# Tiles at other addresses in a decoder trunk: stationary operands at the high end of the large buffers, starts at multiples of 128 bytes

## The chip, the cores and the metric

The kernel runs on one core of a Trainium2 chip. A core has a matrix engine (TensorE, PE in the rows), a vector engine (VectorE, DVE), an activation engine (ScalarE, ACT), GpSimd (POOL) and a queue engine (SyncE, SP) that issues the transfers. They share an on-chip memory of 128 partitions. A tile occupies the same byte range in each partition; its address below is its first byte in the partition. Matmuls write into a second memory, PSUM. The metric is the device time of one execution in microseconds, lower is better.

## The reference

Two layers over 256 tokens of width 1024. Each layer has a feed-forward half, a token mixer and a second feed-forward half, each behind a norm that is shifted, scaled and gated by a vector c:

```python
for l in range(DEPTH):
    mod = (c_act @ w_ada[l] + b_ada[l]).reshape(B, 3, 3, D_MODEL)
    h = ada_norm(x, norm_g[l, 0], mod[:, 0, 0], mod[:, 0, 1])
    x = x + 0.5 * mod[:, 0, 2][:, None, :] * swiglu(h, ffn_w13[l, 0], ffn_w2[l, 0])
    h = ada_norm(x, norm_g[l, 1], mod[:, 1, 0], mod[:, 1, 1])
    x = x + mod[:, 1, 2][:, None, :] * token_mixer(h, w_in[l], ..., w_out[l], cos, sin)
    h = ada_norm(x, norm_g[l, 2], mod[:, 2, 0], mod[:, 2, 1])
    x = x + 0.5 * mod[:, 2, 2][:, None, :] * swiglu(h, ffn_w13[l, 1], ffn_w2[l, 1])
return rms_norm(x, final_g)
```

swiglu is (silu(h @ a) * (h @ b)) @ w2 with an inner width of 2816. token_mixer projects h once, runs three kinds of attention over 16 heads and projects the result back to 1024. All of it is in float32.

## The kernel before

**Products in three parts.** A float32 product is computed from operands that are each split into a high and a low part in the format float32r: hi*hi + hi*lo + lo*hi, three matmuls into the same PSUM bank (`mm3`). Of the activations the split, transposed tiles are the stationary operand: `hThi0`, `hTlo0` for the first 128 tokens (t = 0), `hThi1`, `hTlo1` for the second (t = 1), 8 chunks of 128 columns each, and `gThi`, `gTlo` (three buffers of each, 2 chunks of 128) for the gated inner values. Weights are the moving operand: a chunk of 128 x 1024 is loaded into `raw` (7 buffers), ScalarE copies it to `whi` and VectorE subtracts to `wlo` (8 buffers of each).

**Feed-forward.** The inner width is cut into 11 groups j. `G1(j, t, ks)` multiplies h by a group's two halves, 512 columns, over 8 chunks k; `act` applies silu and the gate; `TR` transposes the result into gThi/gTlo; `G2` multiplies by w2 into y. In the steady loop the tokens alternate inside k:

```python
def steady(j):
    for k in K8:
        for t in range(NT):
            G1(j, t, [k])
    ...
    for f in range(2):
        for t in range(NT):
            G2(j - 1, t, (f,))
    for t in range(NT):
        TR(j, t)
```

So 48 matmuls of G1 take t = 0 and t = 1 in threes by turns, 24 of G2 follow, then four transposes. The last group (`end`) has `G1(j, 1, K8[2:])`, 18 matmuls at t = 1 alone.

**Mixer.** `proj(name, t, K8)` multiplies h by six groups of columns, five of 512 and one (`nv`) of 284, 24 matmuls for each t, and `oproj` projects back (six of its eight chunks from the hT tiles, two from gT tiles). The first projection of the mixer is `proj("ka", 0, K8)`, at t = 0 alone.

**Other names.** `onesr` is a stationary tile of ones that spreads a gate row over the partitions (`mod_part`); `ident` is the moving operand of transposes; `crow` is a row of c by which `raw` is multiplied and summed in `columns`.

**Order.** The code is recorded once, a scheduler fixes each engine's order and every buffer from its own costs and a table of offsets, and the code is run a second time to issue it. Every recorded instruction therefore has one line, that of the issuing loop.

**Place.** `Program.tile` makes a tile at its first use, and the pool lays tiles one behind the other in the order in which they are made. So the order of first use in the code sets the addresses. A tile's size is a multiple of 32 bytes, and small tiles between the large ones move all that follow off the multiples of 128. The built programs place (first byte in the partition; in brackets what is left over from a multiple of 128):

```
                   before                  after
onesr              26688 (64)              25728 (0)
crow               41216 (0)               40192 (0)
hThi0, hTlo0       62112, 66208 (32)       202240, 206336 (0)
raw, 7 buffers     70304 to 98976 (32)     60928 to 89600 (0)
whi, 8 buffers     101216 to 133984 (96)   91648 to 124416 (0)
wlo, 8 buffers     133984 to 166752 (96)   124416 to 157184 (0)
hThi1, hTlo1       174944, 179040 (96)     210432, 214528 (0)
gThi, 3 buffers    187232 to 190304 (96)   218624 to 221696 (0)
gTlo, 3 buffers    190304 to 193376 (96)   221696 to 224768 (0)
nq0, nq1           193376, 197472 (96)     169472, 173568 (0)
ms, 4 buffers      214560 to 220704 (32)   189952 to 196096 (0)
pt, 4 buffers      222208 to 228352 (0)    196096 to 202240 (0)
```

Of the kernel before, what the change touches and what calls it, by code (L numbers as in the profile page):

```python
# [7 lines left out]
F32 = mybir.dt.float32  # L8
F32R = mybir.dt.float32r
# [277 lines left out]
class Program:  # L287
# [9 lines left out]
            k.made = []  # L297

    def tile(self, pool, shape, dt, name, bufs=1, loose=False, psum=False):
        if name not in self.kinds:  # L300
            self.kinds[name] = Kind([pool.tile(shape, dt, name=f"{name}_{i}" if bufs > 1 else name)
                                     for i in range(bufs)], loose)
        kind = self.kinds[name]
        b = Buf(len(self.bufs), kind, psum)
        self.bufs.append(b)
        return View(b, kind.tiles[self.plan[1][b.i] if self.plan else 0])
# [298 lines left out]
GROUPS1 = [2, 2, 2, 1, 1]  # L605
NRAW, NHL, NMS, NPT = 7, 8, 4, 4
S0, S1 = 21, 33


@with_exitstack  # L610
# [1186 lines left out]
```

## Time and profile before

| | |
|---|---|
| median of 3 runs | 1066.04 us (1064.94 to 1066.87) |
| profiled execution, its time | 1065.23 us |
| its span, first to last instruction | 1063.5 us |
| TensorE busy | 1041.4 us |
| VectorE busy | 830.9 us |
| ScalarE busy | 603.3 us |
| bytes moved | 257.97 MB |

The span is what the rows below cover; the time of the same execution is 1.7 us longer, and the median of the runs another 0.8 us. A matmul's row gives its start and a modelled end, and matmuls overlap: the distance between two starts is what a matmul takes from the engine, not the duration in its row.

### The profile page before, as it was taken

To read this page: it belongs to the slowest core of one execution; us is meant where nothing else is said; L and a number is where in the kernel's file an instruction comes from. 1 tells how busy PE (TensorE), PEld (TensorE's weight loads), DVE (VectorE), ACT (ScalarE), POOL (GpSimd) and SP (SyncE) were. 2 spreads that over 40 slices of the span, in tenths; PEclk is the share of its full clock that TensorE was granted. 3 is DMA by queue.
4 is the path that set the end of the run, shared out by engine and by line. 5 is a ranking of instruction groups with operands and counts; after the bars stand their busy time and mean duration, and the time that the engine had idled before them with its cause. 6 is when DMAs were issued, how large, how long until landed. Compare 5 with 4: busy or idle time off the path is not lost.

```text
span 1063.5 us, 14643 instructions
## 1 busy us (share of the span) xinstructions
PE 1041.4 (98%) x5060; PEld 838.7 (79%) x5060; DVE 830.9 (78%) x1561; ACT 603.3 (57%) x1094; POOL 27.7 (3%) x63
## 2 busy tenths in 40 slices
PE   5999999999999999999999999999999999999997
PEld 3888888888777788788888888887877788888885
DVE  6999988779998887788587667758999778556554
ACT  5564354567887644535485444447677766444442
POOL 3000000000000100000000000000000010000000
PEclk9999999999999999999999999999999999999999
DMA  9999999567663698899548777854758247666611
GB/s 341 371 324 367 377 337 327 191 206 243 204 227 123 223 339 318 291 339 336 198 168 283 256 268 257 284 210 154 236 180 264 93 149 277 210 206 210 209 65 39
DMA packets 71468, 257.97 MB, mean 243 GB/s; under 512 B 8193, under 2 KB 8193, under 8 KB 71394
## 3 DMA queue, kind: packets, MB, share of 16 engines
q1 hardware_dynamic: 70850, 256.12, 68.8%
q0 software_dynamic: 544, 0.93, 0.4%
q8 instruction: 39, 0.64, 0.2%
q14 instruction: 35, 0.29, 0.1%
HBM read 255.96 MB, written 1.05 MB: 242 GB/s over the span
## 4 chain that ended last, share of the span: by engine, by line
PE 87%; DVE 7%; DMA 2%; ACT 2%; issue 1%; POOL 1%; SPq 0%; POOLq 0%; DVEq 0%; ACTq 0%
PE ps_pc L561 51%; PE ps_pa L561 15%; PE ps_pb L561 14%; PE ps_tr L561 7%; DVE wlo L561 3%; DMA raw<-in_w_dram 2%; DMA x<-in_x_dram 1%; ACT whi L561 1%; DVE raw L561 1%; DVE nf L561 0%; POOL ss L561 0%; DVE u L561 0%; ACT xn L561 0%; DVE hTlo L561 0%; SPq L561 0%
## 5 line engine op out<-in xcount | busy, mean ns | idle before, releaser
L561 DVE TENSOR_TENSOR wlo<-raw,whi 128x1024 fp32r<-128x1024 f32 (+1 forms) x342 | 410.8, 1216 | 129.0 <-ACT whi L561 127.4
L561 ACT ACTIVATE whi<-raw 128x1024 fp32r<-128x1024 f32 (+1 forms) x342 | 356.7, 1053 | 200.1 <-PE ps_pc L561 107.6
L561 PE MATMUL ps_pc<-whi,hThi 128*128 128x512 f32 (+1 forms) x872 | 347.6, 399 | 0.4 <-ACT gates L561 0.3
L561 PE MATMUL ps_pc<-whi,hTlo 128*128 128x512 f32 (+1 forms) x872 | 340.7, 391 | 0.0
L561 PE MATMUL ps_pc<-wlo,hThi 128*128 128x512 f32 (+1 forms) x872 | 340.5, 390 | 0.0
L561 PEld LDWEIGHTS ps_pc<-whi,hThi 128*128 128x128 f32 x872 | 163.9, 188 | 37.2 <-issue 1.8
L561 PEld LDWEIGHTS ps_pc<-whi,hTlo 128*128 128x128 f32 x872 | 163.7, 188 | 36.7 <-DVE hTlo L561 0.2
L561 PEld LDWEIGHTS ps_pc<-wlo,hThi 128*128 128x128 f32 x872 | 164.0, 188 | 33.3
L561 DVE CUSTOM_DVE_ANT_0 raw<-raw,crow 128x1024 f32<-128x1024 f32 x96 | 115.6, 1221 | 7.2 <-DMA raw<-in_wada_dram 7.2
L561 ACT ACTIVATE gThi<-ps_tr 128x256 fp32r<-128x256 f32 x88 | 32.7, 383 | 74.4 <-PE ps_tr L561 74.2
L561 ACT ACTIVATE sg<-ps_pc 128x256 f32<-128x256 f32 x82 | 31.5, 384 | 75.8 <-PE ps_pc L561 75.5
L561 PE MATMUL ps_pa<-whi,gThi 128*128 128x512 f32 x184 | 73.5, 399 | 0.0
L561 PE MATMUL ps_pb<-whi,gThi 128*128 128x512 f32 x176 | 72.4, 411 | 0.0
L561 PE MATMUL ps_pa<-whi,gTlo 128*128 128x512 f32 x184 | 72.0, 391 | 0.0
L561 PE MATMUL ps_pa<-wlo,gThi 128*128 128x512 f32 x184 | 71.8, 390 | 0.0
L561 PE MATMUL ps_pb<-whi,gTlo 128*128 128x512 f32 x176 | 69.1, 393 | 0.0
L561 PE MATMUL ps_pb<-wlo,gThi 128*128 128x512 f32 x176 | 68.7, 390 | 0.0
L561 DVE SCALAR_TENSOR_TENSOR gate<-raw,cact,gate 128x1024 f32<-128x1024 f32 x48 | 61.4, 1279 | 6.6 <-DMA raw<-in_wada_dram 6.6
L561 ACT ACTIVATE ms<-ms,nm 128x128 f32<-128x128 f32 (+1 forms) x96 | 42.6, 446 | 16.5 <-DVE nm L561 16.5
L561 DVE TENSOR_TENSOR gg<-ps_pc,sg 128x256 f32<-128x256 f32 x82 | 33.5, 420 | 20.8 <-ACT sg L561 19.6
L561 DVE TENSOR_TENSOR gTlo<-ps_tr,gThi 128x256 fp32r<-128x256 f32 x88 | 36.0, 420 | 16.9 <-ACT gThi L561 16.9
L561 PEld LDWEIGHTS ps_pa<-whi,gTlo 128*128 128x128 f32 x184 | 34.5, 188 | 7.5
(257 smaller groups left out, 1085.8 us busy)
## 6 DMA issues: line engine op xcount, KB each, us to landing
raw<-in_w_dram SPq DMA_DIRECT2D x264, 512.0 KB, 4.9
raw<-in_wada_dram SPq DMA_DIRECT2D x144, 512.0 KB, 4.8
raw<-in_win_dram SPq DMA_DIRECT2D x40, 512.0 KB, 4.3
raw<-in_wc_dram SPq DMA_DIRECT2D x16, 512.0 KB, 3.5
raw<-in_wout_dram SPq DMA_DIRECT2D x16, 512.0 KB, 5.1
raw<-in_win_dram SPq DMA_DIRECT2D x4, 426.0 KB, 3.1
x<-in_x_dram SPq DMA_DIRECT2D x2, 512.0 KB, 6.6
out_dram<-xn SPq DMA_DIRECT2D x4, 256.0 KB, 2.1
```

Of the source, the lines that this page charges most:

```text
L561: return getattr(self.eng, op)(*[plain(a) for a in args], **{k: plain(v) for k, v in kw.items()})
```

## The change

All large tiles are made at once, at the first use of any of them, in the order of a list `HOMES`; small tiles follow when they are first used. Since every size in the list is a multiple of 128 bytes, or stands where the next still starts on one, each of the listed tiles starts at a multiple of 128. The transposed inputs (hThi0, hTlo0, hThi1, hTlo1) and the gated tiles (gThi, gTlo) are last in the list, so they lie above all the others. The instructions of each engine, their order and the buffer numbers that they use are the same in both programs.

```diff
     def tile(self, pool, shape, dt, name, bufs=1, loose=False, psum=False):
+        if name not in self.kinds and name in HOMES:
+
+            for n, (s, d, b) in HOMES.items():
+                self.kinds[n] = Kind([pool.tile(s, d, name=f"{n}_{i}" if b > 1 else n) for i in range(b)], False)
         if name not in self.kinds:
...
+HOMES = {
+    "x0": ([128, 1024], F32, 1), "x1": ([128, 1024], F32, 1), "ones": ([128, 128], F32, 1),
...
+    "raw": ([128, 1024], F32, 7), "nf": ([128, 256], F32, 2), "whi": ([128, 1024], F32R, 8),
+    "wlo": ([128, 1024], F32R, 8), "tk": ([128, 4, 512], F32, 1), "sg": ([128, 256], F32, 2),
...
+    "rb": ([128, 8, 16], F32, 1), "ms": ([128, 384], F32, 4), "pt": ([128, 384], F32, 4),
+    "hThi0": ([128, 8, 128], F32R, 1), "hTlo0": ([128, 8, 128], F32R, 1), "hThi1": ([128, 8, 128], F32R, 1),
+    "hTlo1": ([128, 8, 128], F32R, 1), "gThi": ([128, 2, 128], F32R, 3), "gTlo": ([128, 2, 128], F32R, 3),
+}
```

## Rows read from the trace of the kernel before

**Rows 1.** The page's first part: span and busy time of each engine.

```profile
span 1063.5 us, 14643 instructions
...
PE 1041.4 (98%) x5060; PEld 838.7 (79%) x5060; DVE 830.9 (78%) x1561; ACT 603.3 (57%) x1094; POOL 27.7 (3%) x63
```

**Rows 2.** The page's fourth part: the chain that ended last, by engine.

```profile
PE 87%; DVE 7%; DMA 2%; ACT 2%; issue 1%; POOL 1%; SPq 0%; POOLq 0%; DVEq 0%; ACTq 0%
```

**Rows 3.** Chain from 610 to 725 us: start us, us, engine and output, matmuls merged.

```profile
619.88 11.15 PE ps_pc L561 x48
631.03 1.37 PE ps_pa L561 x6
...
633.76 1.36 PE ps_pa L561 x6
...
636.49 0.44 PE ps_tr L561 x4
636.93 11.15 PE ps_pc L561 x48
```

**Rows 4.** The chain from 190 to 235 us, the same columns.

```profile
191.81 1.39 PE ps_pa L561 x6
...
193.42 1.38 PE ps_pc L561 x6
194.80 4.08 PE ps_pa L561 x18
198.88 4.08 PE ps_pc L561 x18
...
216.59 5.60 PE ps_pc L561 x24
```

**Rows 5.** The chain from 1030 us to the end.

```profile
1046.14 4.08 PE ps_pc L561 x18
```

**Rows 6.** TensorE's timeline near 209 us: start us, duration, instruction, merged count.

```profile
209.40 1.09 PE L561 MATMUL ps_tr<-nq,onesr 128*128 128x512 f32 x4
210.33 0.40 PE L561 MATMUL ps_pc<-whi,hThi 128*128 128x512 f32 x1
```

**Rows 7.** Groups of one tile (hThi, then gThi): count, duration min/median/max ns.

```profile
L561 PE MATMUL ps_pc<-whi,hThi x872: 288/393/578, 27.5 to 1049.4; 128*128 128x512 f32 x168, 128*128 128x284 f32 x7
...
L561 PE MATMUL ps_pa<-whi,hThi x40: 389/389/628, 17.8 to 865.4; 128*128 128x512 f32 x40
...
L561 PE MATMUL ps_tr<-whi,hThi x16: 389/394/775, 17.2 to 59.0; 128*128 128x512 f32 x16
...
L561 PE MATMUL ps_pb<-whi,hThi x16: 389/393/482, 22.0 to 62.5; 128*128 128x512 f32 x16
...
L561 PE MATMUL ps_pa<-whi,gThi x184: 389/389/481, 64.0 to 1045.3; 128*128 128x512 f32 x184
...
L561 PE MATMUL ps_pb<-whi,gThi x176: 389/389/481, 66.9 to 1055.1; 128*128 128x512 f32 x176
...
L561 PE MATMUL ps_pc<-whi,gThi x8: 393/474/587, 323.4 to 849.4; 128*128 128x512 f32 x8
```

**Rows 8.** Stretches: length, busy us of each engine (count), clock, DMA share, GB/s.

```profile
20.00:205.00 185.00, 185.00 (x828) 149.69 (x827) 168.55 (x273) 90.37 (x131) 0.55 (x1) 1.00 0.93 342
205.00:350.00 145.00, 143.54 (x854) 115.21 (x853) 131.56 (x369) 112.63 (x272) 4.87 (x6) 1.00 0.59 195
...
535.00:725.00 190.00, 190.00 (x857) 154.97 (x856) 134.05 (x181) 98.31 (x145) 2.10 (x4) 1.00 0.72 244
725.00:860.00 135.00, 133.57 (x807) 105.55 (x806) 117.51 (x353) 101.66 (x250) 3.08 (x4) 1.00 0.53 174
```

**Rows 9.** Groups that write or read raw: count, duration min/median/max ns, forms.

```profile
L561 ACT ACTIVATE whi<-raw x342: 681/1060/1097, 15.1 to 1032.6; 128x1024 fp32r<-128x1024 f32 x169, 128x852 fp32r<-128x852 f32 x2
L561 DVE TENSOR_TENSOR wlo<-raw,whi x342: 731/1221/1228, 16.6 to 1033.6; 128x1024 fp32r<-128x1024 f32 x168, 128x852 fp32r<-128x852 f32 x2, 128x568 fp32r<-128x568 f32 x1
...
L561 DVE CUSTOM_DVE_ANT_0 raw<-raw,crow x96: 1174/1219/1445, 8.9 to 810.8; 128x1024 f32<-128x1024 f32 x96
```

More of the change, by code (lines that the diff above doesn't have):

```diff
@@ L607 @@
 S0, S1 = 21, 33
+HOMES = {
+    "x0": ([128, 1024], F32, 1), "x1": ([128, 1024], F32, 1), "ones": ([128, 128], F32, 1),
+    "ident": ([128, 128], F32, 1), "onesr": ([128, 128], F32R, 1), "mask": ([128, 384], F32, 1),
+    "lower": ([128, 128], F32, 1), "cmask": ([128, 2, 16], F32, 1), "vals": ([128, 2, 12, 64], F32, 1),
+    "fqk": ([128, 2, 8, 66], F32, 1), "kcT": ([128, 2, 16], F32, 1), "kcs": ([128, 2, 2, 16], F32R, 1),
+    "hexp": ([128, 2, 4, 2, 16], F32, 1), "crow": ([128, 1024], F32, 1), "gate": ([128, 1024], F32, 2),
+    "cs": ([128, 2, 2, 16], F32, 1), "xn": ([128, 1024], F32, 1), "zbmo": ([128, 4, 256], F32, 1),
+    "raw": ([128, 1024], F32, 7), "nf": ([128, 256], F32, 2), "whi": ([128, 1024], F32R, 8),
+    "wlo": ([128, 1024], F32R, 8), "tk": ([128, 4, 512], F32, 1), "sg": ([128, 256], F32, 2),
+    "gg": ([128, 256], F32, 2), "nq0": ([128, 4, 256], F32R, 1), "nq1": ([128, 4, 256], F32R, 1),
+    "u": ([128, 512], F32, 2), "nk0": ([128, 2, 256], F32R, 1), "nk1": ([128, 2, 256], F32R, 1),
+    "vbd": ([128, 8, 64], F32, 1), "wc2": ([128, 256], F32, 1), "ra": ([128, 8, 16], F32, 1),
+    "rb": ([128, 8, 16], F32, 1), "ms": ([128, 384], F32, 4), "pt": ([128, 384], F32, 4),
+    "hThi0": ([128, 8, 128], F32R, 1), "hTlo0": ([128, 8, 128], F32R, 1), "hThi1": ([128, 8, 128], F32R, 1),
+    "hTlo1": ([128, 8, 128], F32R, 1), "gThi": ([128, 2, 128], F32R, 3), "gTlo": ([128, 2, 128], F32R, 3),
+}
 @with_exitstack
```

## The prediction

> **What bounds the kernel now.** I read the busy shares first: TensorE is busy for 1041.4 of 1063.5 us, VectorE for 830.9 and ScalarE for 603.3 [rows 1]. A busy TensorE may still have gaps that its modelled ends hide, so I went on to the chain of work that ended last. It runs through TensorE for 87% of the span [rows 2]. So the time is made of the distances from one matmul to the next, and the question is what sets such a distance. No row has it directly, but the chain merges matmuls that follow each other without a wait into one piece with a count. The length of a piece divided by its count is the mean distance.
>
> The steady loop of the feed-forward blocks shows two levels side by side. The 48 matmuls of G1 take 11.15 us, 232.3 ns each. The matmuls of G2 that follow, six to a piece, take 1.36 or 1.37 us, 227 to 228 ns each [rows 3]. Both kinds have the same shape: 128 rows of weights, 512 moving columns, the same moving tiles whi and wlo. At the full clock, 2.4 GHz, 512 columns would alone be 213 ns. The clock was granted fully in every stage listed [rows 8].
>
> What differs is the stationary operand. G1 uses hThi0/hTlo0 and hThi1/hTlo1 by turns (t alternates inside k), G2 uses gThi/gTlo. Where the program uses one of them alone, the levels come apart. The 24 matmuls of the mixer's first projection at t = 0 take 5.60 us, **233.3 ns** each. The 18 at t = 1 in the end of the first feed-forward block (G1(j, 1, K8[2:])) take 4.08 us, **226.7 ns** each. The 18 of G2 just before them also take 4.08 us, 226.7 ns [rows 4]. The end of the last block shows the same 4.08 us for 18 at t = 1, 850 us later [rows 5]. Code, shape and moving tiles are the same for t = 0 and t = 1; the data and the place of the stationary tiles are not. By the placement table hThi0 and hTlo0 lie at 62,112 to 70,304 bytes of a partition, hThi1 and hTlo1 at 174,944 to 183,136, and gThi and gTlo at 187,232 to 193,376. A third low tile agrees: onesr, at 26,688, is the stationary operand of four matmuls that take 0.93 us from the first start to the next instruction's start, 232.5 ns each [rows 6]. Two other pieces show that the fast level is not reached at once. The first six matmuls of G2 after a t = 0 stretch take 1.39 us (231.7 each), the first six at t = 1 behind transposes 1.38 us (230 each) [rows 4].
>
> **The change, part by part.** No instruction is added, taken away or moved; every tile gets another address. I cost this by kind of tile.
>
> *Stationary tiles.* All twelve go to 202,240 to 224,768 bytes, above the tiles that are fast now. Counts: matmuls with whi and hThi are 872 + 40 + 16 + 16 = 944 [rows 7], and each comes with one of wlo and hThi and one of whi and hTlo, 2832 in all. Of these 96 have 284 columns (eight chunks, two t, two layers, three each), which leaves 2736 of 512 columns, 1368 for each t. With gThi there are 184 + 176 + 8 = 368 [rows 7], so 1104. In the program's own order 676 of the t = 0 matmuls have no t = 1 matmul among the three wide matmuls before them, 692 have one; 802 of the t = 1 matmuls have a t = 0 one there, 566 have none. The 676 run at 233.3 ns, the 692 + 802 at the mixed 232.3 ns. If all of them settle at the 226.7 ns that the high tiles show, the change gives 676 x 6.6 ns = 4.5 us and 1494 x 5.6 ns = 8.4 us, **12.8 us** together. The 566 and the 1104 are there already: nothing.
>
> *Settling.* After transposes or other small matmuls the first six of a series cost 230 to 231.7 ns, 0.02 to 0.03 us above level per series. Today G1's series don't settle at all, so this cost is not separate; afterwards each has it once. With 40 series of G1 in four blocks and some few in the mixers I take **1 us** back (bounds 0 and 2).
>
> *Where TensorE waits for others.* A faster matmul gains nothing where the next one waits for VectorE or ScalarE anyway. In the steady block from 535 to 725 us and in the first one TensorE shows no idle time; in the mixers it is idle 1.5 us of 145 and 1.4 us of 135, with VectorE at 91% and 87% there [rows 8]. The mixers hold 624 of the 2736 matmuls (five projections and oproj, two t, two layers), so they hold about 2.9 us of the 12.8. I take half of that as lost, **1.5 us** (bounds 0 and 2.9).
>
> *Moving tiles.* whi and wlo go from 101,216 to 166,752 down to 91,648 to 157,184. Eight slots of each lie over 65 KiB of a partition now, and G1's pieces of 48, which use changing slots, show no spread (11.15 us twice) [rows 3]. So nothing, with the reservation that the lowest slots reach some 9,500 bytes lower than any whi did.
>
> *VectorE, ScalarE, DMA.* They read and write tiles that move from 32 or 96 bytes past a multiple of 128 to a multiple. whi<-raw takes 1060 ns and wlo<-raw,whi 1221 ns in the median, the product of raw and crow, summed, where crow already starts at a multiple of 128, 1219 ns [rows 9]. I see no price of the residue between the last two and take nothing; TensorE's work would cover some per cent either way.
>
> Sum: 12.8 - 1.0 - 1.5 = 10.3 us. The span of 1063.5 becomes 1053.2, the profiled execution's 1065.2 becomes 1054.9. The median of the three runs is 1066.0, 0.8 above that execution, so I forecast **1055.7 us**. Its own range is 1051.5 (all 12.8 and a little of the series that restart slowly today) to 1058.5 (both deductions at their upper bound).
>
> A rule stands against both halves of the change. The Trainium skill, SBUF — State Buffer, gives no price to a place in the partition: under Who interferes with whom TensorE never waits on anyone, and under Specifications lines are 16 bytes, so that all starts of before, multiples of 32, would count as aligned. By it the sum is 0. The distances of rows 4, 5 and 6 disagree on the place, and nothing here speaks against it on the alignment, to which I give no term either.
>
> **The rivals.**
>
> *Partly lost* (12%). The first block loads at 0.93 of the DMA engines' time [rows 8]; if its loads, not TensorE, would set its pace as soon as TensorE is 2% faster, its 528 matmuls give nothing (some 2.8 us), and the mixers' 2.9 us may go too: a gain of 12.8 - 1.0 - 5.7 = 6.1 us, 1059.9. Against it: TensorE is not seen idle from 20 to 205 us.
>
> *The place doesn't matter* (9%): the difference between t = 0 and t = 1 comes from the data or from what else runs at that time. Then no change, 1066.0. For it: only three low tiles and two groups of high ones can be compared. Against it: the pieces of t = 0 and t = 1 lie 18 us apart in the same code.
>
> *The new place is slow* (7%). What counts may be the residue and not the distance: hT0 starts at 32 past a multiple of 128, onesr at 64, all the fast tiles at 96. A start at 0 has no row; if it were slow too, or the last 22 KiB were a slow stretch of their own, all 3840 would run at 233.3: 1494 x 1.0 + (566 + 1104) x 6.6 = 12.5 us more, 1078.5. It decides from a distance of 230.0 ns on, the mean over all 3840 today. For it: the confounding is complete in the rows. Against it: 64 and 32 being equally slow and 96 alone fast is an odd rule of alignment, while the addresses order the levels plainly.
>
> *More* (2%): the higher place also lowers the 226.7; every nanosecond on 3840 is 3.8 us, so 1050 or less.
>
> **How the numbers follow.** The forecast gets 70%. Within 0.2% (2.1 us), about what a measurement of this kernel can tell from no change, lies the second rival: same 0.09. Slower 0.07, faster 0.70 + 0.12 + 0.02 = 0.84. A range from 1050.5 to 1062.0 takes the forecast whole, most of the first rival and leaves out the two of no gain, some 17 to 18 in a hundred.
>
> **What would show it.** The chain's pieces of 48 matmuls of G1 at 10.9 us instead of 11.15; the 24 of the first projection at 5.44 instead of 5.60; those at t = 1 and of G2 unchanged at 4.08 for 18. Durations of whi<-raw and wlo<-raw,whi unchanged. If G1 falls to 10.9 and the span falls by less than 8 us, idle time of TensorE in the mixers or in the first block has grown. If t = 1 and G2 rise above 230 ns each, the new place is slow. The prediction is wrong if 48 matmuls of G1 stay at 11.15.

## The result, and the profile after

The changed kernel takes 1057.57 us (median of 4 runs, 1056.55 to 1058.31), the kernel before 1066.39 us on the same chip (median of 4, 1064.94 to 1066.87). The ratio is 0.9919, with a 95% interval from 0.9902 to 0.9936: faster by 8.8 us. The forecast was 1055.7 us in a range from 1050.5 to 1062.0. The number came out well. Its cause did not, and that the number held in spite of it was luck: the experiments below show that the place of the stationary tiles, on which the prediction rests, has no price.

The page's first part shows the difference on TensorE. Its busy time falls by 9.3 us from [rows 1], that of the other engines by under 1 us:

```profile
span 1055.6 us, 14643 instructions
...
PE 1032.1 (98%) x5060; PEld 838.0 (79%) x5060; DVE 830.0 (79%) x1561; ACT 603.1 (57%) x1094; POOL 27.7 (3%) x63
```

The page's fourth part, the chain by engine, still runs through TensorE, with VectorE's share grown from 7% to 10% [rows 2]:

```profile
PE 83%; DVE 10%; issue 2%; ACT 2%; DMA 2%; POOL 1%; POOLq 0%; DVEq 0%; ACTq 0%
```

The chain from 600 to 725 us (start us, us, engine and output, matmuls merged) answers to [rows 3]. 48 matmuls of G1 take 10.94 or 10.93 us where they took 11.15; the pieces of G2 are all at 1.36:

```profile
616.01 10.94 PE ps_pc L565 x48
626.94 1.36 PE ps_pa L565 x6
628.30 1.36 PE ps_pb L565 x6
629.66 1.36 PE ps_pa L565 x6
...
632.39 0.44 PE ps_tr L565 x4
632.82 10.93 PE ps_pc L565 x48
```

The chain from 188 to 235 us answers to [rows 4]. The 24 at t = 0 fall from 5.60 to 5.49, and the 18 at t = 1 stay at 4.08. Two series that follow other instructions begin unsettled, that is, above the level that they reach after some matmuls: the six at 1.40, and the 24, which at 226.7 ns each would be 5.44:

```profile
189.70 1.36 PE ps_pa L565 x6
...
191.35 1.40 PE ps_pc L565 x6
192.75 4.11 PE ps_pa L565 x18
196.86 4.08 PE ps_pc L565 x18
...
214.57 5.49 PE ps_pc L565 x24
```

TensorE's timeline near 207 us answers to [rows 6]. onesr, still low, takes 0.94 us from its first start to the next instruction's, 235 ns each, although it now starts at a multiple of 128 bytes like the rest; the next matmuls, with hThi0, follow 0.23 us apart:

```profile
207.35 1.10 PE L565 MATMUL ps_tr<-nq,onesr 128*128 128x512 f32 x4
208.29 0.39 PE L565 MATMUL ps_pc<-whi,hThi 128*128 128x512 f32 x1
208.52 0.39 PE L565 MATMUL ps_pc<-wlo,hThi 128*128 128x512 f32 x1
```

The groups of raw answer to [rows 9]: the same durations within 2 ns in the median.

```profile
L565 ACT ACTIVATE whi<-raw x342: 662/1061/1072, 15.2 to 1024.9; 128x1024 fp32r<-128x1024 f32 x169, 128x852 fp32r<-128x852 f32 x2
L565 DVE TENSOR_TENSOR wlo<-raw,whi x342: 731/1219/1228, 16.5 to 1026.0; 128x1024 fp32r<-128x1024 f32 x168, 128x852 fp32r<-128x852 f32 x2, 128x568 fp32r<-128x568 f32 x1
...
L565 DVE CUSTOM_DVE_ANT_0 raw<-raw,crow x96: 1168/1217/1446, 9.1 to 805.5; 128x1024 f32<-128x1024 f32 x96
```

Since all of TensorE's instructions are the same in both traces, each distance between two starts can be compared with the same distance before. Between matmuls of 512 columns that wait in neither trace, those at t = 0 give 6.2 us, those at t = 1 3.4 and those with gThi/gTlo 0.2: 9.8 us. Waits of TensorE take 1.9 us back: 1.7 between a wide matmul and the transposes or small matmuls behind it, 0.2 elsewhere. That leaves 7.9, the difference of the two spans, 1063.5 and 1055.6, and of the times of the two profiled executions, 1065.23 and 1057.34. The medians differ by a little more.

Most of the new waits stand in the second feed-forward block. From 350 to 535 us TensorE is busy for 183.00 us, 1.34 less than the 184.34 that the kernel before had there. Its waits for gg from VectorE grew there from 0.6 to 2.0 us. Most of that lies between 415 and 440 us, where it waited for nothing before. The first fence is the waits of TensorE in that stretch (waiter, what it waited for: us in total, times, longest). The second is the chain in the same stretch: gg stands behind the product of raw and crow and the wlo before it, which waited 2.65 us for whi, and whi for a load of raw that landed at 417.2 us. So for a moment the loads set the pace, as the rival "Partly lost" had it for the first block. The third and the fourth are rows by windows with the columns of [rows 8], first of the kernel before, then of the changed one. In the mixers (205 to 350 and 725 to 860 us) TensorE is idle for 1.57 and 1.44 us, as before within 0.2.

```profile
PE ps_tr L565 <- DVE gg L565: 1.4, 2, 1.1
```

```profile
410.59 6.63 DMA raw<-in_w_dram
...
417.33 1.07 ACT whi L565
...
419.56 1.22 DVE raw L565
...
420.79 0.67 DVE gg L565 x2
```

```profile
350.00:535.00 185.00, 184.34 (x825) 149.00 (x824) 143.85 (x195) 90.62 (x128) 2.71 (x4) 1.00 0.82 292
```

```profile
205.00:350.00 145.00, 143.43 (x855) 115.49 (x854) 132.00 (x367) 112.35 (x271) 5.84 (x8) 1.00 0.60 197
350.00:535.00 185.00, 183.00 (x831) 149.49 (x830) 144.48 (x198) 92.04 (x131) 1.78 (x2) 1.00 0.80 288
...
725.00:860.00 135.00, 133.56 (x807) 105.93 (x806) 117.50 (x353) 102.62 (x252) 2.52 (x3) 1.00 0.56 184
```

### The profile page after: what moved, and what is told of

It reads as the page before. It is cut to its first block, busy times and chain, and to the rows that moved or that the text cites. A ratio compares the mean times of both kernels' runs of the same rounds, so it can differ in the third digit from the quotient of the medians.

```text
span 1055.6 us, 14643 instructions
## 1 busy us (share of the span) xinstructions
PE 1032.1 (98%) x5060; PEld 838.0 (79%) x5060; DVE 830.0 (79%) x1561; ACT 603.1 (57%) x1094; POOL 27.7 (3%) x63
## 4 chain that ended last, share of the span: by engine, by line
PE 83%; DVE 10%; issue 2%; ACT 2%; DMA 2%; POOL 1%; POOLq 0%; DVEq 0%; ACTq 0%
PE ps_pc L565 49%; PE ps_pa L565 14%; PE ps_pb L565 14%; PE ps_tr L565 7%; DVE wlo L565 4%; DVE raw L565 2%; DMA raw<-in_w_dram 1%; ACT whi L565 1%; DVE gate L565 1%; DVE nf L565 1%; DMA raw<-in_wada_dram 1%; POOL ss L565 0%; DVE gg L565 0%; DVE u L565 0%; POOL gate L565 0%
## 5 line engine op out<-in xcount | busy, mean ns | idle before, releaser
L565 PE MATMUL ps_pc<-wlo,hThi 128*128 128x512 f32 (+1 forms) x872 | 337.1, 387 | 0.0
L565 ACT ACTIVATE ms<-ms,nm 128x128 f32<-128x128 f32 (+1 forms) x96 | 42.6, 445 | 16.0 <-DVE nm L565 15.9
```

Source lines behind the costliest of these rows:

```text
L565: return getattr(self.eng, op)(*[plain(a) for a in args], **{k: plain(v) for k, v in kw.items()})
```

## The experiments

The theory at first was the prediction's: a low stationary tile costs about 233 ns per matmul, a high one 226.7 (place theory). The rival was the other half of the change, the residue: starts at multiples of 128 help. After the first four runs both had fallen, and a third took their place. The kernels change nothing but the list of homes or a spare tile, so instructions, order and data are those of the changed kernel. Each ratio is to runs of the kernel before on the same chip. In the cuts the lists are wrapped anew, so that only tiles that move or are added are marked, and "..." stands for what is left out.

**1. Stationary tiles low, starts still at multiples of 128.**

```diff
 HOMES = {
+    "hThi0": ([128, 8, 128], F32R, 1), "hTlo0": ([128, 8, 128], F32R, 1), "hThi1": ([128, 8, 128], F32R, 1),
+    "hTlo1": ([128, 8, 128], F32R, 1), "gThi": ([128, 2, 128], F32R, 3), "gTlo": ([128, 2, 128], F32R, 3),
     "x0": ([128, 1024], F32, 1), "x1": ([128, 1024], F32, 1), "ones": ([128, 128], F32, 1),
...
-    "hThi0": ([128, 8, 128], F32R, 1), "hTlo0": ([128, 8, 128], F32R, 1), "hThi1": ([128, 8, 128], F32R, 1),
-    "hTlo1": ([128, 8, 128], F32R, 1), "gThi": ([128, 2, 128], F32R, 3), "gTlo": ([128, 2, 128], F32R, 3),
```

> The same list of tiles, with hThi0 to gTlo put first instead of last: 16,512 to 41,088 bytes of a partition, every start still a multiple of 128. Place theory (a stationary tile that lies low costs about 233 ns per matmul of 512 columns, one that lies high 226.7): all 3840 wide matmuls at about 233, so 12.5 us above before and 21 us above the changed kernel, about 1079 us; the chain's pieces of 48 matmuls of G1 at 11.2 us and the 18 of G2 or of t = 1 at 4.20 instead of 4.08. Rival (the residue counts, starts at multiples of 128 are what helps): as the changed kernel, 1057.6 us, 48 of G1 at 10.93.

Measured: 1071.99 us (median of 5), ratio to before 1.0054 (1.0041 to 1.0066). The chain of this kernel, 188 to 235 us and then 600 to 725 us:

```profile
199.57 4.19 PE ps_pc L565 x18
...
217.42 5.58 PE ps_pc L565 x24
...
607.28 11.16 PE ps_pc L565 x48
```

Everything is on the upper level, as the place theory wants; a residue of 0 by itself doesn't help. The time is 7 us under the 1079 expected. The span grew by 6.8 us, which is the sum of 2.8 at t = 1, 3.8 for gThi/gTlo, -0.5 at t = 0 and 0.7 of waits: before, t = 1 and gThi/gTlo ran at 230.3 and 228.7 ns in the mean, with their unsettled matmuls, and not at 226.7, and the level here is nearer 232.5 than 233.3.

**2. Stationary tiles high, 32 past a multiple of 128.**

```diff
+    "spare": ([128, 8], F32, 1),
     "hThi0": ([128, 8, 128], F32R, 1), "hTlo0": ([128, 8, 128], F32R, 1), "hThi1": ([128, 8, 128], F32R, 1),
```

> The changed kernel with a spare tile of 32 bytes ahead of hThi0, so that hThi0 to gTlo stay high (202,272 to 224,800 bytes) but all start at 32 past a multiple of 128, which is the residue that hThi0 and hTlo0 had before. Place theory: as the changed kernel, 1057.6 us within 2 us, 48 of G1 at 10.93 us. Rival (residue): all of them at about 233 ns, 1078 us, 48 of G1 at 11.2.

Measured: 1073.43 us (median of 5), ratio 1.0069 (1.0057 to 1.0082). The chain of this kernel from 860 to 1060 us:

```profile
882.61 5.59 PE ps_pc L565 x24
901.21 11.20 PE ps_pc L565 x48
```

48 of G1 take 11.20 us, with the tiles 32 bytes from where the change puts them. The place theory is refuted. So is the residue on its own, since in the first experiment 0 was no better.

**3. Stationary tiles in the middle, whi and wlo at the top.**

```diff
-    "raw": ([128, 1024], F32, 7), "nf": ([128, 256], F32, 2), "whi": ([128, 1024], F32R, 8),
-    "wlo": ([128, 1024], F32R, 8), "tk": ([128, 4, 512], F32, 1), "sg": ([128, 256], F32, 2),
+    "raw": ([128, 1024], F32, 7), "nf": ([128, 256], F32, 2), "tk": ([128, 4, 512], F32, 1),
...
+    "gTlo": ([128, 2, 128], F32R, 3), "whi": ([128, 1024], F32R, 8), "wlo": ([128, 1024], F32R, 8),
```

> hThi0 to gTlo at 136,704 to 159,232 bytes, below whi and wlo, which go to the top (159,232 to 224,768). Where between 70,000 and 175,000 bytes a stationary tile gets slower has no row yet. Place theory with a step below 136,700: as the changed kernel, 1057.6 us, 48 of G1 at 10.93. With a step above 159,000: all at about 233, 1079 us. A slope over the address (about 6.6 ns per 110,000 bytes): some 2 ns more for each of 3840 matmuls, 1064 to 1067 us, 48 of G1 at about 11.0. Rival (what counts is whether stationary or moving tiles lie higher, not the address): 1079 us.

Measured: 1057.87 us (median of 5), ratio 0.9923 (0.9910 to 0.9935), as the changed kernel. The chain from 600 to 725 us:

```profile
616.76 10.94 PE ps_pc L565 x48
```

**4. whi and wlo low, stationary tiles where the change put them.**

```diff
 HOMES = {
+    "whi": ([128, 1024], F32R, 8), "wlo": ([128, 1024], F32R, 8),
     "x0": ([128, 1024], F32, 1), "x1": ([128, 1024], F32, 1), "ones": ([128, 128], F32, 1),
...
-    "whi": ([128, 1024], F32R, 8), "wlo": ([128, 1024], F32R, 8),
     "tk": ([128, 4, 512], F32, 1), "sg": ([128, 256], F32, 2),
```

> The changed kernel with whi and wlo moved to the low end (16,512 to 82,048 bytes); hThi0 to gTlo stay where the change put them. Theory (only the stationary operand's place counts): as the changed kernel, 1057.6 us within 2 us, 48 of G1 at 10.93. Rival (the moving operand's place counts too, low is slow): up to 6.6 ns more on each of 3840 matmuls, up to 1083 us, 48 of G1 at up to 11.2.

Measured: 1072.12 us (median of 5), ratio 1.0058 (1.0044 to 1.0072). The chain, 188 to 235 and 600 to 725 us:

```profile
200.32 4.19 PE ps_pc L565 x18
...
218.15 5.60 PE ps_pc L565 x24
...
606.50 11.19 PE ps_pc L565 x48
```

The stationary tiles haven't moved, and their matmuls are on the upper level. So it is not a property of the stationary tile alone. What orders the kernels so far is the **difference of the two starts**, moving less stationary, left over from a multiple of 256:

```
kernel, stationary tiles        whi        stationary   left over   level
before, hThi0                   101216      62112        192        upper
before, hThi1                   101216     174944          0        lower
before, gThi                    101216     187232          0        lower
before, onesr (moving: nq0)     193376      26688         32        upper
changed, hThi0                   91648     202240          0        lower
changed, onesr (moving: nq0)    169472      25728        128        upper
1, hThi0                        114176      16512        128        upper
2, hThi0                         91648     202272        224        upper
3, hThi0                        159232     136704          0        lower
4, hThi0                         16512     202240        128        upper
```

Buffers and chunks of these tiles lie multiples of 512 apart, so one row speaks for all buffers of a pair of tiles. This is the pair theory of the runs that follow.

**5. Low again, but matched.** The first experiment, with 128 bytes between the stationary tiles and the rest.

```diff
     "hTlo1": ([128, 8, 128], F32R, 1), "gThi": ([128, 2, 128], F32R, 3), "gTlo": ([128, 2, 128], F32R, 3),
+    "spare": ([128, 32], F32, 1),
     "x0": ([128, 1024], F32, 1), "x1": ([128, 1024], F32, 1), "ones": ([128, 128], F32, 1),
```

> The first experiment's list (hThi0 to gTlo low, at 16,512 to 39,040 bytes) with a spare of 128 bytes behind gTlo. That moves whi, wlo and all else up by 128, so that the start of every whi and wlo lies a multiple of 512 above that of every hThi to gTlo (there it was 384 past a multiple of 512). Pair theory (what counts is the difference of the moving and the stationary tile's starts, left over from a multiple of 512: at 0 a matmul settles at 226.7 ns, at other values about 233): as the changed kernel, 1057.6 us within 2 us, 48 of G1 at 10.93 us. Place theory (a low stationary tile is slow, whatever the difference): as the first experiment, 1072 us, 48 of G1 at 11.16.

Measured: 1058.13 us (median of 5), ratio 0.9925 (0.9913 to 0.9937). 14 us lie between this kernel and the first experiment, whose stationary tiles have the same addresses. The chain, 188 to 235 and 600 to 725 us:

```profile
196.81 4.08 PE ps_pc L565 x18
...
214.72 5.48 PE ps_pc L565 x24
...
617.17 10.93 PE ps_pc L565 x48
```

**6. The kernel before and one spare tile.** No list of homes, no operand of these matmuls moved to the high end, none of them at a multiple of 128.

```diff
--- before
     def tile(self, pool, shape, dt, name, bufs=1, loose=False, psum=False):
+        if name not in self.kinds and name == "raw":
+            pool.tile([128, 80], F32, name="spare")
         if name not in self.kinds:
```

> The kernel before, with one spare tile of 320 bytes made ahead of raw: hThi0 and hTlo0 stay at 62,112 to 70,304, everything above them moves up by 320 bytes, which makes the difference of whi or wlo to hThi0 and hTlo0 a multiple of 512 too (it was 192 past one) and keeps it for hThi1, hTlo1, gThi, gTlo. No large tile of these starts at a multiple of 128. Pair theory: the whole gain of the change, 1057.6 us within 2 us, first projection (24 at t = 0) at 5.45 to 5.49 us, 48 of G1 at 10.93. Place theory: as before, 1065.6 us, 5.60 and 11.15 us.

Measured: 1058.50 us (median of 5), ratio 0.9927 (0.9915 to 0.9940): the whole gain of the change within what can be measured. hThi0 and hTlo0 lie where they lay in the kernel before, at 62,112, and their 24 matmuls went from 5.60 to 5.49 us because whi and wlo moved up by 320 bytes. The chain, 188 to 235 and 600 to 725 us (lines are numbered differently in this kernel):

```profile
216.09 5.49 PE ps_pc L563 x24
...
601.29 10.93 PE ps_pc L563 x48
```

**7. Three differences in one kernel.** 256 at t = 0, 64 at t = 1, 96 for gThi and gTlo.

```diff
+    "spare0": ([128, 64], F32, 1),
     "hThi0": ([128, 8, 128], F32R, 1), "hTlo0": ([128, 8, 128], F32R, 1),
+    "spare1": ([128, 48], F32, 1),
     "hThi1": ([128, 8, 128], F32R, 1), "hTlo1": ([128, 8, 128], F32R, 1),
+    "spare2": ([128, 120], F32, 1),
     "gThi": ([128, 2, 128], F32R, 3), "gTlo": ([128, 2, 128], F32R, 3),
```

> The changed kernel with spares that set three differences (moving start less stationary start, left over from a multiple of 512): 256 for hThi0 and hTlo0, 64 for hThi1 and hTlo1, 96 for gThi and gTlo. Pair theory with a period of 512: nothing is fast, some 1073 us, the 24 of the first projection at 5.60. With a period of 256: those 24 at 5.45 to 5.49 us, G1 by turns 11.15, G2 and t = 1 at 4.19 for 18, about 1070 us. With a period of 32 or 64 bytes nothing fits the runs so far. Place theory: as the changed kernel, 1057.6.

Measured: 1067.54 us (median of 11), ratio 1.0013 (1.0004 to 1.0021). The chain, 188 to 235 us, has G2 (ps_pa), then t = 1, then t = 0, and G1 from 600 us on mixes t = 0 and t = 1:

```profile
194.78 4.20 PE ps_pa L565 x18
198.98 4.14 PE ps_pc L565 x18
...
216.80 5.49 PE ps_pc L565 x24
...
604.40 11.13 PE ps_pc L565 x48
```

The 24 at a difference of 256 are as at 0, so the period is 256 bytes or a divisor; since a difference of 128 was slow in experiments 1 and 4, it is 256. At 96 a matmul takes 233.3 ns; at 64 the 18 take 230.0 each, less than at 96 and more than at 0.

**8. wlo alone 128 off.**

```diff
+    "spare0": ([128, 32], F32, 1),
     "wlo": ([128, 1024], F32R, 8), "tk": ([128, 4, 512], F32, 1), "sg": ([128, 256], F32, 2),
...
+    "spare1": ([128, 96], F32, 1),
     "hThi0": ([128, 8, 128], F32R, 1), "hTlo0": ([128, 8, 128], F32R, 1), "hThi1": ([128, 8, 128], F32R, 1),
```

> The changed kernel with wlo alone moved by 128 bytes against the rest: whi to hThi to gTlo at a difference of a multiple of 512, wlo 128 past one. Each three matmuls hold one with wlo. Pair theory, each matmul for itself: one in three is slow, 226.7 + 2.1 = 228.8 ns in the mean, 1065 us, 48 of G1 at 11.0. If one slow one unsettles the others, as t = 0 and t = 1 by turns ran at 232.3: 1070 to 1073 us, 48 of G1 at 11.15. If wlo's place has no part in it (whi alone is what counts): 1057.6 us, 10.93.

Measured: 1071.95 us (median of 5), ratio 1.0052 (1.0038 to 1.0066). The chain, 600 to 725 us:

```profile
608.64 11.19 PE ps_pc L565 x48
...
625.87 11.10 PE ps_pc L565 x48
```

One pair in three that doesn't match costs as much as three: 233.1 and 231.3 ns per matmul in these pieces, where experiment 4 has 11.19 us for 48. By the starts in the trace, the distance to the next matmul is 234.4 ns in the mean from whi with hThi at t = 0 and t = 1, 233.0 from wlo with hThi and 230.5 from whi with hTlo, so the two matched ones are slow as well. The price isn't an amount for each matmul on its own.

**9. The two steps of 32 not yet seen.** 32 at t = 0, 160 at t = 1, and 0 for gThi and gTlo.

```diff
+    "spare0": ([128, 56], F32, 1),
     "hThi0": ([128, 8, 128], F32R, 1), "hTlo0": ([128, 8, 128], F32R, 1),
+    "spare1": ([128, 32], F32, 1),
     "hThi1": ([128, 8, 128], F32R, 1), "hTlo1": ([128, 8, 128], F32R, 1),
+    "spare2": ([128, 40], F32, 1),
     "gThi": ([128, 2, 128], F32R, 3), "gTlo": ([128, 2, 128], F32R, 3),
```

> The changed kernel with spares for the two differences not yet seen in steps of 32 (moving start less stationary start, left over from a multiple of 256): 32 for hThi0 and hTlo0, 160 for hThi1 and hTlo1, and 0 for gThi and gTlo as a reference. So far 0 settles at 226.7 ns, 64 at 229.0, 96, 192 and 224 at 233.0 to 233.3, 128 near 232. If 0 is the one good value: the 24 of the first projection at 5.55 to 5.60 us, 48 of G1 at 11.1 to 11.2, G2 at 4.08 for 18, some 1068 us. If the price falls off from 0 to both sides or another value is better than 0: 32 at or below 229, the 24 at 5.50 or less.

Measured: 1067.63 us (median of 11), ratio 1.0011 (1.0002 to 1.0021). The chain, 188 to 235 us (t = 0), 600 to 725 us (G2, then G1), and 1020 us to the end (t = 1):

```profile
217.80 5.58 PE ps_pc L565 x24
...
602.15 1.36 PE ps_pa L565 x6
...
605.31 11.11 PE ps_pc L565 x48
...
1048.97 4.21 PE ps_pc L565 x18
```

With this run every step of 32 within 256 has a value. The middle column is a piece of the chain above or in [rows 4]; the last is worked out from the starts in the trace, a third of the distance over three matmuls, the median where nine or more matmuls of one kind follow each other without a wait:

```
difference   piece of the chain            ns each   median, ns
0            4.08 us for 18 (changed)      226.7     226.7
32           5.58 for 24 (run 9)           232.5     233.3
64           4.14 for 18 (run 7)           230.0     229.0
96           4.20 for 18 (run 7)           233.3     233.3
128          4.19 for 18 (run 4)           232.8     232.0
160          4.21 for 18 (run 9)           233.9     234.0
192          5.60 for 24 (before)          233.3     233.3
224          11.20 for 48 (run 2)          233.3     233.0 to 233.7
```

None is better than 0.

**10. whi and wlo low, but matched.** The fourth experiment with 128 bytes ahead of hThi0.

```diff
+    "spare": ([128, 32], F32, 1),
     "hThi0": ([128, 8, 128], F32R, 1), "hTlo0": ([128, 8, 128], F32R, 1), "hThi1": ([128, 8, 128], F32R, 1),
```

> The fourth experiment's list (whi and wlo low, at 16,512 to 82,048 bytes, hThi0 to gTlo at the high end) with a spare of 128 bytes ahead of hThi0, which makes the difference a multiple of 256 where it was 128 past one. Pair theory: as the changed kernel, 1057.6 us within 2 us, 48 of G1 at 10.93 us. Rival (the moving tiles' low place is what cost 14 us there): 1072 us, 11.19.

Measured: 1057.81 us (median of 5), ratio 0.9919 (0.9907 to 0.9932). The moving tiles' place has no price either. The chain, 600 to 725 us:

```profile
600.17 10.93 PE ps_pc L565 x48
```

**11. Which of a matmul's neighbours counts.** hThi and gThi matched to whi; hTlo and gTlo matched to wlo, 128 away.

```diff
+    "spare0": ([128, 32], F32, 1),
     "wlo": ([128, 1024], F32R, 8),
...
-    "hThi0": ([128, 8, 128], F32R, 1), "hTlo0": ([128, 8, 128], F32R, 1), "hThi1": ([128, 8, 128], F32R, 1),
-    "hTlo1": ([128, 8, 128], F32R, 1), "gThi": ([128, 2, 128], F32R, 3), "gTlo": ([128, 2, 128], F32R, 3),
+    "spare1": ([128, 32], F32, 1),
+    "hThi0": ([128, 8, 128], F32R, 1), "hThi1": ([128, 8, 128], F32R, 1), "gThi": ([128, 2, 128], F32R, 3),
+    "spare2": ([128, 32], F32, 1),
+    "hTlo0": ([128, 8, 128], F32R, 1), "hTlo1": ([128, 8, 128], F32R, 1), "gTlo": ([128, 2, 128], F32R, 3),
```

> In the three matmuls of a product (whi with hThi, wlo with hThi, whi with hTlo) the next matmul's weights are loaded while the present one streams its moving tile. Here hThi and gThi are matched to whi, and wlo, hTlo and gTlo all lie 128 past that (left over from a multiple of 256). So each moving tile is matched to the stationary tile that is loaded next: whi then hThi, wlo then hTlo, whi then hThi. Each matmul's own pair is matched in one of three only (wlo with hThi and whi with hTlo are 128 apart). If the pair that counts is the streaming tile and the weights being loaded: as the changed kernel, 1057.6 us within 2 us, 48 of G1 at 10.93. If it is a matmul's own two tiles, or both: as with wlo alone moved, about 1072 us, 11.1 to 11.2.

Measured: 1066.44 us (median of 11), ratio 1.0001 (0.9992 to 1.0011). The chain, 600 to 725 us:

```profile
604.71 11.09 PE ps_pc L565 x48
```

Neither expectation holds. 231.0 ns each is well above the matched 227.7 (10.93 for 48) and not above the pieces of experiment 8, though two of three matmuls have their own pair unmatched here and one of three there. So matching only the weights that are loaded next isn't enough. It isn't without effect either: the time is 5.5 us under that of experiment 8. In both experiments the starts of whi and wlo also differ by 128 past a multiple of 256, which they do in no other kernel here; whether that has a part in it was not tried. Which accesses meet stays open.

## Why the prediction was right in its number and wrong in its cause

**What bounds the kernel.** Right: the distance between matmuls sets the time, it has two levels in the kernel before, and the change moves G1 from one to the other. The 9.8 us gained, before waits, lie in those distances.

**The step that failed** is "What differs is the stationary operand", with its conclusion that the levels go by the tile's height in the partition. The rows [rows 4 to 6] were read rightly, but height was one of several things in which these tiles differed. The prediction saw one of them, the residue of the stationary tile's own start, called the confounding complete, and set it aside as an odd rule. The moving tile's address, which it had in the same table, never entered: 101,216 less 62,112 is 192 past a multiple of 256, 101,216 less 174,944 and less 187,232 are 0 past one. Experiments 1 against 5 and 4 against 10 change that difference by 128 bytes while no tile moves by more than 128, and 14 us come or go. Experiment 6 gives the gain without the list.

**The main term**, 12.8 us, stood because the change happens to make all these differences multiples of 256: from whi to hThi0 it is 110,592 bytes, 432 times 256. That was luck. Where all starts are multiples of 128 the difference is 0 or 128, and of the four such arrangements without a spare two had 0 (the changed kernel and experiment 3) and two had 128 (experiments 1 and 4, at 1072 us). So the rival with the time on the other side, "The new place is slow", was nearer to an even chance than to the 7% that it got; its mechanism, the stationary tile's own residue, is refuted as well.

**Settling** was put too low. 12.8 less the 9.8 measured is 3.0 us, where 1 was taken with a bound of 2. In the trace of the changed kernel the first six distances of a series (wide matmuls without a wait or another instruction between them) take 231.3 ns in the mean, the next three 229.1 and those behind 226.8, so that short series hardly reach the lower level. The mixers show it most: their distances fell by 1.0 us, where the prediction counted 2.9 of the 12.8. It shared these out evenly, though by its own rates mainly the t = 0 half of their 624 matmuls, some 2.1 us, stood to gain; in the mixers those without a t = 1 matmul just before them went from 233.3 to 229.9 ns, not to 226.7.

**Where TensorE waits.** 1.5 us were taken for the mixers. Their waits grew by 0.1 us; of the 1.9 us that went to waits 1.3 fell to the second block, nearly all to the wait for gg, and the prediction gave that block no term. The two deductions together were 2.5 and measured 4.9.

**Slips that changed little.** The stationary tiles are ten, not twelve. The sixteen buffers of whi and wlo lie over 64 KiB, not 65. With both deductions at their upper bound the sum gives 1058.1, not 1058.5.

**Moving tiles, VectorE, ScalarE, DMA.** Nothing was taken, and nothing was seen: durations within 2 ns, and experiments 3 and 10 at 1057.87 and 1057.81 with whi and wlo at either end.

**The rule weighed.** By the Trainium skill, SBUF — State Buffer, Specifications (TRN2), lines are 16 bytes, so that starts that are multiples of 32 should be alike, and by it the sum was 0. The trace disagrees, though not in the way supposed: 32 bytes on the stationary tiles alone (experiment 2) cost 15.9 us against the changed kernel, and the address of one tile by itself decides nothing.

**Which part of the change works.** Neither the high end nor the multiples of 128 as such, only the differences that came out of the list. The one spare tile of experiment 6 does the same (1058.50, its interval overlapping the changed kernel's). No version was found that beats the changed kernel: 0 is the best of the eight differences, and the matched kernels lie from 1057.57 to 1058.50.

**Open:** why the difference counts, and between which of the accesses; experiments 8 and 11 speak against a price for each matmul on its own and against one that the next weights alone decide, and don't settle more. Steps below 32 bytes and matmuls of other shapes weren't tried.

## What to carry to other kernels

Where long series of matmuls bound a kernel, divide the chain's pieces by their counts; if one shape has two levels, tabulate the start addresses of both operands, and look at their differences before looking at either address. Here a spare tile of 320 bytes, which makes moving less stationary start a multiple of 256 for every pair of the wide matmuls, gave 0.7% with no instruction changed. And when a table of addresses seems to order a measurement plainly, list every other quantity that the same table orders as well, and move one of them alone.

## What the hardware showed that was not expected

- The distance between float32r matmuls of 512 columns depends on the difference of the moving and the stationary tile's starts, left over from a multiple of 256: 226.7 ns at 0, 229.0 at 64, about 232 at 128, 233.0 to 234.0 at the five other steps of 32. The mean granted clock was 0.997 to 0.999 in all these runs.
- One unmatched pair in three was enough to lose the lower level for all three (experiment 8: 11.19 and 11.10 us for 48, where the matched kernels have 10.93), as t = 0 and t = 1 by turns did before [rows 3].
- The lower level isn't reached at once: six matmuls behind transposes take 1.40 us where six settled ones take 1.36, and in the mean over the changed kernel's series the distance is 231.3 ns for the first six, 229.1 for the next three and 226.8 behind them.
